# Eight column chunks by seven block products instead of five, each with its own operand distance, and accumulating DMAs for the low halves

## The chip, the core and the metric

The kernel runs on one core of a Trainium2 chip. The metric is the device time of one execution in microseconds (us), lower is better. A core has five engines with queues of their own: PE (TensorE, matrix products), DVE (VectorE), ACT (ScalarE), POOL (GpSimd) and SP (SyncE, which here issues DMAs). Each works through its queue in order; semaphores tie the queues together.

## The reference

One layer of a transformer block on 512 tokens of width 1024, in float32: two kinds of attention, an output projection, then a gated feed-forward part. The change concerns that last part alone:

```python
def conv_glu(x, w_up, conv_w, conv_b, w_down):      # x: 512 x 1024 (normalised)
    hid = x @ w_up                                   # 512 x 5632: 2816 gate, 2816 up columns
    hid = causal_depthwise_conv(hid, conv_w, width=3) + conv_b
    gate, up = hid[..., :2816], hid[..., 2816:]
    return (jax.nn.silu(gate) * up) @ w_down         # 2816 x 1024
```

## The kernel before

Float32 products are made of three matmuls each: both operands are split into a high part (`hi`, rounded to the fast fp32r type) and a low part (`lo`, the rest), and hi·hi, hi·lo and lo·hi are added up in PSUM.

**The up projection** runs in 22 chunks, `up0` to `up21`. A chunk holds 128 gate and 128 up columns; its weights are stationary, the transposed tokens (`hth`, `htl`) move. A chunk of the old form (`up_body`) takes 2 × 8 products of K = 128 with 512 moving columns, times three: 48 matmuls. A chunk named in `SEVEN` takes another way (`up_seven`): its weights and the tokens are seen as 2 × 2 blocks, and seven block products of 256 moving columns (4 × 3 matmuls each, 84 in all) stand for the eight, as in Strassen's scheme. The sums of token blocks (`ts`, four tiles) are made once; the sums of weight blocks are made for each such chunk by DVE in `block_sums` (tile `sx`) and split in `split_seven` into `wxh` and `wxl`. The products `p1`, `p5`, `p7`, `p6` leave by copies (`pc`, `hg`) and adds (`hu`, `hg`), which also set free the PSUM banks that the next chunk starts in.

The tiles of stationary weights (`whi`, `wlo`, `wxh`, `wxl`) are a little larger than needed, so that their used part can begin some elements behind the tile's start: 16 elements (64 bytes) for the sevens and for up0 and up1, 48 for some chunks of the attention, 0 for the rest. What is called the distance here is where the stationary operand starts minus where the moving one starts, modulo 256 bytes.

**The pairs.** The outputs of two chunks form a pair, 11 in all; a pair's blocks and their sums become the stationary operands of the down projection, `ax` (2048 wide: 1024 high, 1024 low) and `ay` (1536 wide: 768 and 768). `pair_sums(i)` makes four sums on DVE (into `st`, a tile with one buffer, and back into `ub`), then `halves` makes each high half by a copy on ACT (L908) and each low half by a subtraction on DVE (L909), in pieces of 768, 256, 256 and 512 columns. There is room for eight `ax`, but not for all `ay`: those of pairs 0 to 6 are stored to DRAM (`ayd`, L933, POOL's DMA queue) and fetched later by `fetch` (L953, also POOL). `ax8` lies in a `ts` buffer and `ay8` in the one of `wxh`, once the last seven is done.

**The down projection** takes 11 chunks `dn0_i` (which use `ax`) and then 11 `dn1_i` (which use `ay`); their weights are split in the same way, and their body runs `steps0` or `steps1` on the side: the sums of the last two pairs and fetches.

**What sets the order.** `run_chunk` interleaves a chunk's products with the split of the next chunk's weights (`split_gen`), piece by piece. The weights of the chunk after next are loaded (SP, 1 MB into one of two `raw` buffers) when a split ends; if the next chunk but one is a seven, its `block_sums` follow. A scheduler orders each engine's queue from the dependencies.

Of the kernel before, what the change touches and what calls it, by code (L numbers as in the profile page):

```python
# [8 lines left out]
F32 = mybir.dt.float32  # L9
F32R = mybir.dt.float32r  # L10
AF = mybir.ActivationFunctionType
ALU = mybir.AluOpType
# [3 lines left out]
P = 128  # L16
S = 512
# [42 lines left out]

CHUNKS = _chunks()

SEVEN = (5, 8, 11, 14, 17)


@with_exitstack
def block_kernel(ctx: ExitStack, tc: tile.TileContext, x, xt, params, g2, rbx, wts, wd0, wd1, out):
    nc = tc.nc
    V, A, G, PE, SP = nc.vector, nc.scalar, nc.gpsimd, nc.tensor, nc.sync
# [39 lines left out]
    raws, splits, late = {}, {}, {"halves": (), "casts": (), "products": ()}  # L109
    FIRST_DN = order.index("dn0_0")  # L110
    keep = {}
# [58 lines left out]
    def is_seven(i):  # L170
        return i < len(order) and order[i] in [f"up{j}" for j in SEVEN]

# [15 lines left out]
    def split_seven(i, raw, hi, lo):  # L188

        key = order[i]  # L190
        wh, wl = (late["pool"].tile([P, 1600], F32R, tag=tag, name=f"{tag}_{key}")[:, 16:1552]
                  for tag in ("wxh", "wxl"))
        splits[key] = tuple(t.rearrange("p (k c) -> p k c", c=P) for t in (hi, lo, wh, wl))
        sx = late["sx"]
        for j, (h, l, src) in enumerate(((hi[:, 0:1024], lo[:, 0:1024], raw[:, 0:1024]),
                                         (wh[:, 0:1024], wl[:, 0:1024], sx[:, 0:1024]),
                                         (hi[:, 1024:2048], lo[:, 1024:2048], raw[:, 1024:2048]),
                                         (wh[:, 1024:1536], wl[:, 1024:1536], sx[:, 1024:1536]))):
            A.copy(h, src)
            V.tensor_tensor(l, src, h.bitcast(F32), op=ALU.subtract)  # L200
            if j < 3:
                yield

    def split_gen(i, pieces):

        if i >= len(order):
            return
        key = order[i]
        kn = CHUNKS[i][1]
        raw = raws.pop(i)  # L210
        sh = 48 if key[:2] in ("qA", "kA", "vA", "vB") else 16 if key in ("up0", "up1") or is_seven(i) else 0
        n = 512 * kn if i >= FIRST_DN else 2048
        hi = wp.tile([P, 2112], F32R, tag="whi", name=f"whi_{key}")[:, sh:sh + n]
        lo = wp.tile([P, 2112], F32R, tag="wlo", name=f"wlo_{key}")[:, sh:sh + n]
        splits[key] = (hi.rearrange("p (k c) -> p k c", k=kn), lo.rearrange("p (k c) -> p k c", k=kn))
        if i >= FIRST_DN:
            yield from split_down(i - FIRST_DN, raw, hi, lo)
        elif is_seven(i):
            yield from split_seven(i, raw, hi, lo)
        n = 2048 // pieces  # L220
        for j in range(pieces if i < FIRST_DN and not is_seven(i) else 0):
            sl = slice(n * j, n * (j + 1))
            if i == 0 and j == 0:
                V.tensor_copy(hi[:, sl], raw[:, sl])
            else:
                A.copy(hi[:, sl], raw[:, sl])  # L226
            E = G if i == 2 else V
            E.tensor_tensor(lo[:, sl], raw[:, sl], hi[:, sl].bitcast(F32), op=ALU.subtract)  # L228
            if j < pieces - 1:
                yield  # L230


        nxt = {0: None, 1: i + 3, 2: None}.get(i - FIRST_DN, i + 2)
        if nxt is not None and nxt < len(order):
            next(load(nxt))
        yield
        if is_seven(i + 1):
            yield from block_sums(i + 1)
# [3 lines left out]
    def run_chunk(key, body, pieces=4):  # L242

        sp = split_gen(pos[key] + 1, pieces)
        for _ in body(*splits.pop(key)):
            next(sp, None)
            yield
        for _ in sp:
            pass
# [12 lines left out]
    pp = ctx.enter_context(tc.tile_pool(name="pp", bufs=1, space=PSUM))  # L262
    dram = ctx.enter_context(tc.tile_pool(name="dram", bufs=1, space=bass.MemoryType.DRAM))
    htd = dram.tile([NT, 2, P, S], F32, tag="htd", name="htd")
    ayd = dram.tile([7, P, 1536], F32, tag="ayd", name="ayd")


    reset = pool_c.tile([P, S], F32, tag="reset", name="reset")
# [560 lines left out]
    hi, lo = splits.pop("wo3")  # L829
# [8 lines left out]
    fp = late["pool"] = ctx.enter_context(tc.tile_pool(name="fp", bufs=1))  # L838
# [5 lines left out]
    pairs = {}  # L844
# [19 lines left out]
    def gate(j, pg):  # L864
        g = fp.tile([P, S], F32, tag="cg", name=f"cg{j}", bufs=1)
        conv(pg, j, g)
        A.activation(g, g, AF.Silu)
        return g

    def pair_sums(i):  # L870

        u0, u1 = ub[:, 2 * i % 4, :], ub[:, 2 * i % 4 + 1, :]
        u = ub[:, 2 * i % 4:2 * i % 4 + 2, :].rearrange("p a b -> p (a b)")
        lo_, hi_ = slice(0, 256), slice(256, 512)
        t = {}
        if i < 8:
            ax = fp.tile([P, 2048], F32R, tag="ax", name=f"ax{i}", bufs=8)
            ay = fp.tile([P, 1536], F32R, tag="ay", name=f"ay{i}")
        elif i == 8:

            ax = fp.tile([P, 2048], F32R, tag="ts", name=f"ax{i}", bufs=4)
            ay = fp.tile([P, 1600], F32R, tag="wxh", name=f"ay{i}")[:, 0:1536]
            keep[0] = fp.tile([P, S], F32, tag="hg", name="t2_0")
        else:

            ax = late["hp"].tile([P, 2048], F32R, tag=f"ax{i}", name=f"ax{i}")
            ay = late["hp"].tile([P, 1536], F32R, tag=f"ay{i}", name=f"ay{i}")
        pairs[i] = (ax, ay)

        def sums():  # L890
            t["st"] = st = fp.tile([P, 768], F32, tag="st", name=f"st{i}", bufs=1)
            s1, s42 = st[:, 0:256], st[:, 256:768]
            if i == 9:

                s42 = fp.tile([P, S], F32, tag="cg", name="s42_9", bufs=1)
            s4, s2 = s42[:, 0:256], s42[:, 256:512]
            t["s42"] = s42
            ins = [V.tensor_tensor(s1, u0[:, hi_], u1[:, hi_], op=ALU.add),
                   V.tensor_tensor(u0[:, hi_], u0[:, lo_], u0[:, hi_], op=ALU.subtract),
                   V.tensor_tensor(s2, s1, u0[:, lo_], op=ALU.subtract),  # L900
                   V.tensor_tensor(s4, u1[:, lo_], s2, op=ALU.subtract)]
            return ins

        def halves(a, parts):
            ins, n = [], a.shape[-1] // 2
            for o, src in parts:
                sl = slice(o, o + src.shape[-1])
                A.copy(a[:, sl], src)  # L908
                ins.append(V.tensor_tensor(a[:, n + o:n + sl.stop], src, a[:, sl].bitcast(F32), op=ALU.subtract))  # L909
            return ins  # L910
        return (sums, lambda: halves(ax, ((0, u[:, 0:768]), (768, t["st"][:, 0:256]))),
                lambda: halves(ay, ((0, u[:, 768:1024]), (256, t["s42"]))))

    def keep_place(i):
# [8 lines left out]
    def up_fin(j, pg, pu, g=None):  # L923
        if g is None:
            g = gate(j, pg)
        u = ub[:, j % 4, :]
        conv(pu, NF + j, u)
        late["fin"] = (V.tensor_tensor(u, g, u, op=ALU.mult),)
        if j % 2 == 1 and j // 2 < 9:
            for step in pair_sums(j // 2):  # L930
                step()
            if j // 2 < 7:
                G.dma_start(ayd[j // 2], pairs[j // 2][1].bitcast(F32))  # L933

    def up_body(j):
        def body(hi, lo):
# [10 lines left out]

    def fetch(i):

        tag = {0: "sx", 1: "wxl"}.get(i, "ts" if i < 5 else "ax")  # L950
        n, bufs = {"sx": (1536, 1), "wxl": (1600, 1), "ts": (2048, 4), "ax": (2048, 8)}[tag]
        ay = fp.tile([P, n], F32R, tag=tag, name=f"ay{i}", bufs=bufs)[:, 0:1536]
        G.dma_start(ay, ayd[i])  # L953
        pairs[i] = (pairs[i][0], ay)
# [3 lines left out]
    ts = {}  # L958
# [92 lines left out]
    for j in range(NF):  # L1051
        body = up_first(j) if j < 2 else up_seven(j) if j in SEVEN else up_body(j)
        for _ in run_chunk(f"up{j}", body, pieces=4 if j < 2 else 2):
            pass
        if j == 18:
            for i in range(5):
                fetch(i)


# [110 lines left out]
    def steps0():  # L1170
        yield
        for i in (9, 10):
            ss[i] = pair_sums(i)
            yield from late_pair(ss[i][:2])
            fetch(i - 4)

    def steps1():
        tmp["x"] = [fp.tile([P, 2, D], F32, tag="ax", name=f"x_{r}", bufs=8) for r in range(2)]
# [7 lines left out]
    for s in range(2):  # L1186
        steps = (steps0, steps1)[s]()
        for i in range(NP - 2 * s):
            for _ in run_chunk(f"dn{s}_{i}", down_body(s, i), pieces=2):
                pass  # L1190

    for _ in split_gen(pos[f"dn1_{NP - 1}"], 2):
        pass
# [13 lines left out]
def _layout(inputs):  # L1207
# [12 lines left out]
    for i, (key, kn, parts) in enumerate(CHUNKS[:-2 * NP]):  # L1220
        views = [f[name][0][r0:r0 + kn * P, c0:c0 + n] for name, r0, c0, n in parts]
        w = views[0] if len(views) == 1 else np.concatenate(views, axis=1)
        if key in [f"up{j}" for j in SEVEN]:

# [26 lines left out]
```

## Time and profile before

| | |
|---|---|
| median of 3 runs | 726.53 us (726.07 to 726.63) |
| the profiled execution | 726.66 us, its span 724.9 us |
| granted clock of TensorE | 1.000 |
| up2 to up21 | 402.8 to 615.6 us of the span |
| dn0_0 to the end | from 615.6 us |
| DMA in all | 100.9 MB, 139 GB/s over the span |

Busy times of an engine are sums of durations of its instructions. Since matmuls are pipelined, one lasts longer than the distance to the next one's start. A row of the page's groups gives line, engine, operation, output and inputs, shapes and count, then busy us and mean ns, then the idle time ahead and what ended it. A row of a timeline gives start, duration, engine and line. The chain that ended last tells which work the end of the span hung on.

### The profile page before, as it was taken

The page shows a single profiled execution, that of the slowest core. Times are in us where ns is not written, and L with a number is a line of the kernel's source. Part 1 is how long each engine was busy: PE and PEld are TensorE (multiplying, and loading weights), DVE is VectorE, ACT ScalarE, POOL GpSimd, SP SyncE. Part 2 cuts the span into 40 slices and gives each one's busy share as a digit, 9 for nine tenths or more (in the row PEclk, how much of TensorE's full clock was granted, in tenths as well). Part 3 has the DMA queues.
Part 4 walks back from the last instruction along what each step waited for, and adds up shares of the span by engine and source line. Part 5 has one row for each costly group of instructions (what it writes and reads, how often), then busy time and mean ns, then how long its engine had stood idle before and what let it go on. Part 6 is the DMA issues. An engine that isn't in the chain of part 4 may idle for free.

```text
span 724.9 us, 10589 instructions
## 1 busy us (share of the span) xinstructions
PE 718.6 (99%) x4019; PEld 627.5 (87%) x4019; DVE 565.4 (78%) x1030; ACT 401.5 (55%) x727; POOL 53.6 (7%) x95
## 2 busy tenths in 40 slices
PE   8999999999999999999999999999999999999997
PEld 8999998888988888888889889889898988888886
DVE  6678867775988888566275799998979985997686
ACT  6675656657767676442254556655545653543541
POOL 2701200000101011000012000000000100000000
PEclk9999999999999999999999999999999999999999
DMA  8632232211313111314536613544335553564563
GB/s 308 250 131 78 83 117 74 74 59 58 118 63 113 59 59 59 136 68 144 195 149 239 203 62 156 186 135 160 118 145 186 181 184 117 173 243 174 177 222 116
DMA packets 24786, 100.91 MB, mean 139 GB/s; under 512 B 2592, under 2 KB 7328, under 8 KB 17184
## 3 DMA queue, kind: packets, MB, share of 16 engines
q1 hardware_dynamic: 21792, 87.00, 33.8%
q0 software_dynamic: 2656, 13.11, 5.0%
q8 instruction: 31, 0.51, 0.3%
q14 instruction: 19, 0.16, 0.1%
q10 hardware_dynamic: 288, 0.14, 0.1%
HBM read 88.44 MB, written 11.80 MB: 138 GB/s over the span
## 4 chain that ended last, share of the span: by engine, by line
PE 98%; DMA 1%; SPq 0%; DVE 0%; ACT 0%; DVEq 0%; issue 0%
PE P L1087 14%; PE p L998 7%; PE pg L254 4%; PE pg L253 4%; PE pg L255 4%; PE pu L254 4%; PE pu L255 4%; PE pu L253 4%; PE qkB L255 2%; PE gB L255 2%; PE qkB L253 2%; PE gA L253 2%; PE gA L254 2%; PE gB L253 2%; PE gA L255 2%; PE qkB L254 2%
## 5 line engine op out<-in xcount | busy, mean ns | idle before, releaser
L253 PE MATMUL pg<-hth,whi_up 128*128 128x512 f32 (+1 forms) x152 | 55.7, 367 | 0.0
L255 PE MATMUL pg<-hth,wlo_up 128*128 128x512 f32 (+1 forms) x152 | 55.7, 366 | 0.0
L254 PE MATMUL pg<-htl,whi_up 128*128 128x512 f32 (+1 forms) x152 | 55.7, 366 | 0.0
L254 PE MATMUL pu<-htl,whi_up 128*128 128x512 f32 (+1 forms) x152 | 55.6, 366 | 0.0
L253 PE MATMUL pu<-hth,whi_up 128*128 128x512 f32 (+1 forms) x152 | 55.6, 366 | 0.0
L255 PE MATMUL pu<-hth,wlo_up 128*128 128x512 f32 (+1 forms) x152 | 55.6, 365 | 0.0
L1087 PE MATMUL P<-whi_dn,ax 128*128 128x512 f32 x176 | 54.4, 389 | 0.0
L149 ACT CAST whi_dn<-raw_dn 128x1024 fp32r<-128x1024 f32 x33 | 34.3, 1051 | 25.5 <-PE P L1087 15.2
L145 DVE TENSOR_TENSOR wlo_dn<-raw_dn,whi_dn 128x1024 fp32r<-128x1024 f32 x33 | 40.0, 1224 | 9.2 <-ACT whi_dn L149 9.1
L228 DVE TENSOR_TENSOR wlo_up<-raw_up,whi_up 128x1024 fp32r<-128x1024 f32 (+1 forms) x40 | 41.2, 1062 | 7.0 <-ACT whi_up L226 7.0
L226 ACT CAST whi_up<-raw_up 128x1024 fp32r<-128x1024 f32 (+1 forms) x40 | 34.5, 917 | 14.7 <-PE pu L254 7.9
L1087 PE MATMUL P<-whi_dn,ay 128*128 128x512 f32 x132 | 40.8, 389 | 0.0
L1087 PEld LDWEIGHTS P<-whi_dn,ax 128*128 128x128 f32 x176 | 33.0, 188 | 6.8
L1087 PE MATMUL P<-wlo_dn,ax 128*128 128x512 f32 x88 | 34.2, 389 | 0.0
L254 PEld LDWEIGHTS pu<-htl,whi_up 128*128 128x128 f32 x152 | 28.6, 188 | 4.7
L253 PEld LDWEIGHTS pu<-hth,whi_up 128*128 128x128 f32 x152 | 28.5, 188 | 4.7
L255 PEld LDWEIGHTS pg<-hth,wlo_up 128*128 128x128 f32 x152 | 28.6, 188 | 4.7
L255 PEld LDWEIGHTS pu<-hth,wlo_up 128*128 128x128 f32 x152 | 28.5, 188 | 4.6
L253 PEld LDWEIGHTS pg<-hth,whi_up 128*128 128x128 f32 x152 | 28.6, 188 | 4.6
L254 PEld LDWEIGHTS pg<-htl,whi_up 128*128 128x128 f32 x152 | 28.6, 188 | 4.5
L633 DVE TENSOR_TENSOR_SCAN aB<-aB,reset 128x127 f32<-128x127 f32 (+3 forms) x32 | 26.0, 817 | 6.7 <-ACT aB L628 6.7
L1087 PEld LDWEIGHTS P<-whi_dn,ay 128*128 128x128 f32 x132 | 24.8, 188 | 5.1
(303 smaller groups left out, 2240.3 us busy)
## 6 DMA issues: line engine op xcount, KB each, us to landing
raw_up<-in_wts SPq DMA_DIRECT2D x22, 1024.0 KB, 4.8
raw_dn<-in_wd SPq DMA_DIRECT2D x11, 1024.0 KB, 4.8
raw_dn<-in_wd SPq DMA_DIRECT2D x11, 512.0 KB, 3.4
ayd<-ay POOLq DMA_DIRECT2D x7, 768.0 KB, 5.2
ay<-ayd POOLq DMA_DIRECT2D x7, 768.0 KB, 6.5
raw_gA<-in_wts SPq DMA_DIRECT2D x4, 1024.0 KB, 4.7
raw_qkB<-in_wts SPq DMA_DIRECT2D x4, 1024.0 KB, 4.8
raw_gB<-in_wts SPq DMA_DIRECT2D x4, 1024.0 KB, 4.7
```

Source lines behind the costliest of these rows:

```text
L145: chain("halves", V.tensor_tensor(o, x, y, op=op))
L149: chain("casts", A.copy(hi[:, sl], src))
L226: A.copy(hi[:, sl], raw[:, sl])
L228: E.tensor_tensor(lo[:, sl], raw[:, sl], hi[:, sl].bitcast(F32), op=ALU.subtract)
L253: PE.matmul(ps, sh, mh, start=first, stop=False)
L254: PE.matmul(ps, sh, ml, start=False, stop=False)
L255: PE.matmul(ps, sl, mh, start=False, stop=last)
L633: V.tensor_tensor_scan(ar, ar, reset[:, S - n:S - 1][:, ::-1], 1.0, op0=ALU.mult, op1=ALU.max)
L998: PE.matmul(ps, st, mv[:, k, :], start=first and k == 0 and n == 0, stop=last and k == 3 and n == 2, skip_group_check=True)
L1087: chain("products", PE.matmul(dst, st, mv, start=first and n == 0, stop=last and n == 2, skip_group_check=True))
```

## The change

`SEVEN` goes from five chunks to eight, every second one from up8 on. Each has its own shift of the stationary operand in its tile, from 4 to 56 elements (`BEHIND`, 16 to 224 bytes); chunks that aren't sevens keep theirs. In the built program all moving operands of these products start at one place modulo 256 bytes, and so do the tiles of the stationary ones, so that the shift is the distance.

The low halves of pairs 0 to 8 are no longer subtracted by DVE: ACT writes −src, rounded to fp32r, into the low half's place (that is minus the high half), and a DMA on POOL's queue with `accum_op=add` adds src to it. That makes four such DMAs per pair, 36 in all, of 128, 128, 256 and 384 KB.

With more sevens the `ts`, `wxh` and `sx` tiles are in use until up20, so that buffers move: pair 8 gets an `ax` and an `ay` buffer like the others; for that `ax0` is stored to DRAM (`axd`, 1 MB) and reloaded into a `ts` buffer after up20, and `ay7` is stored too. The fetches come after up20 (0 and 1), after the down chunks 1, 3, 5, 7, 9 (2, 6, 7, 3, 4) and after dn1_0 (5). In code:

```diff
-SEVEN = (5, 8, 11, 14, 17)
+SEVEN = (5, 8, 10, 12, 14, 16, 18, 20)
+BEHIND = dict(zip(SEVEN, (4, 8, 12, 20, 24, 28, 40, 56)))
 def split_seven(i, raw, hi, lo):
-    wh, wl = (late["pool"].tile([P, 1600], F32R, tag=tag, name=f"{tag}_{key}")[:, 16:1552]
+    sh = BEHIND[int(key[2:])]
+    wh, wl = (late["pool"].tile([P, 1600], F32R, tag=tag, name=f"{tag}_{key}")[:, sh:sh + 1536]
...
-    sh = 48 if key[:2] in ("qA", "kA", "vA", "vB") else 16 if key in ("up0", "up1") or is_seven(i) else 0
+    sh = 48 if key[:2] in ("qA", "kA", "vA", "vB") else 16 if key in ("up0", "up1") else BEHIND[int(key[2:])] if is_seven(i) else 0
...
-    ayd = dram.tile([7, P, 1536], F32, tag="ayd", name="ayd")
+    ayd = dram.tile([8, P, 1536], F32, tag="ayd", name="ayd")
+    axd = dram.tile([P, 2048], F32, tag="axd", name="axd")
...
 def pair_sums(i):
-        if i < 8:
+        if i < 9:
             ax = fp.tile([P, 2048], F32R, tag="ax", name=f"ax{i}", bufs=8)
             ay = fp.tile([P, 1536], F32R, tag="ay", name=f"ay{i}")
-        elif i == 8:
-            ax = fp.tile([P, 2048], F32R, tag="ts", name=f"ax{i}", bufs=4)
-            ay = fp.tile([P, 1600], F32R, tag="wxh", name=f"ay{i}")[:, 0:1536]
-            keep[0] = fp.tile([P, S], F32, tag="hg", name="t2_0")
...
+                lo = a[:, n + o:n + sl.stop]
                 A.copy(a[:, sl], src)
-                ins.append(V.tensor_tensor(a[:, n + o:n + sl.stop], src, a[:, sl].bitcast(F32), op=ALU.subtract))
+                if i < 9:
+                    A.activation(lo, src, AF.Copy, scale=-1.0)
+                    G.dma_start(lo, src, accum_op=ALU.add)
+                else:
+                    ins.append(V.tensor_tensor(lo, src, a[:, sl].bitcast(F32), op=ALU.subtract))
...
-            if j // 2 < 7:
+            if j // 2 < 8:
                 G.dma_start(ayd[j // 2], pairs[j // 2][1].bitcast(F32))
+            if j // 2 == 6:
+                G.dma_start(axd, pairs[0][0].bitcast(F32))
...
     def fetch(i):
-        tag = {0: "sx", 1: "wxl"}.get(i, "ts" if i < 5 else "ax")
+        tag = {0: "sx", 1: "wxl", 2: "wxh"}.get(i, "ts" if i < 6 else "ax")
...
-        if j == 18:
-            for i in range(5):
+        if j == SEVEN[-1]:
+            keep[0] = fp.tile([P, S], F32, tag="hg", name="t2_0")
+            ax0 = fp.tile([P, 2048], F32R, tag="ts", name="ax0_", bufs=4)
+            G.dma_start(ax0, axd)
+            pairs[0] = (ax0, None)
+            for i in range(2):
                 fetch(i)
...
-            fetch(i - 4)                      # in steps0
...
+            n = ({1: 2, 3: 6, 5: 7, 7: 3, 9: 4}, {0: 5})[s].get(i)
+            if n is not None:                 # behind each chunk of the down projection
+                fetch(n)
```

Three places show what this makes of the queues. First POOL's queue at pair 0, as it stands now; `ay0<-ub`, `ax0<-st0` and the like are accumulations into the low half, `axd` and `ayd` the places in DRAM:

```order
L912 DMA ay0_4439<-ub_4185 128x256
L912 DMA ax0_4438<-st0_4440 128x256
L912 DMA ax0_4438<-ub_4185 128x768
L941 DMA axd_109<-ax0_4438 128x2048
L912 DMA ay0_4439<-st0_4440 128x512
L938 DMA ayd_108<-ay0_4439 128x1536
L912 DMA ax1_4604<-st1_4606 128x256
```

Before, only the store `ayd<-ay0` stood there, with that of pair 1 right behind it. The store of ax0, written for pair 6 in the code, now stands ahead of pair 0's last accumulation, the one that reads `st0`.

Second DVE's queue in up5, before; `st1` is the tile of pair 1's sums, `p6_5` the bank of up5's product p6:

```order
L1010 TENSOR_TENSOR pc5_4697<-pc5_4697 128x256
L854 SCALAR_TENSOR_TENSOR ub_4184<-pu4_4621,par_88,ub_4184 128x510
L1013 TENSOR_TENSOR hu5_4699<-p6_5_4696,pc5_4697 128x256
L898 TENSOR_TENSOR st1_4601<-ub_4184 128x256
L909 TENSOR_TENSOR ay1_4600<-ub_4184,ay1_4600 128x256
L853 SCALAR_TENSOR_TENSOR cg4_4654<-pg4_4620,par_88,cg4_4654 128x511
L899 TENSOR_TENSOR ub_4184<-ub_4184 128x256
```

And the same place of the changed kernel:

```order
L858 SCALAR_TENSOR_TENSOR ub_4185<-pu4_4630,par_88,ub_4185 128x510
L1018 TENSOR_TENSOR pc5_4706<-pc5_4706 128x256
L897 TENSOR_TENSOR st1_4606<-ub_4185 128x256
L1021 TENSOR_TENSOR hu5_4708<-p6_5_4705,pc5_4706 128x256
L857 SCALAR_TENSOR_TENSOR cg4_4663<-pg4_4629,par_88,cg4_4663 128x511
L898 TENSOR_TENSOR ub_4185<-ub_4185 128x256
```

The subtractions into `ay1` are gone from the queue, and the first sum of pair 1, which writes `st1` into the one buffer that `st0` had, stands ahead of the add that reads `p6_5`; it stood behind it.

Third POOL's queue from pair 8 on, now; `ax0_` is the reloaded tile:

```order
L912 DMA ay8_6061<-ub_4185 128x256
L961 DMA ay0_6394<-ayd_108 128x1536
L912 DMA ax8_6060<-st8_6062 128x256
L912 DMA ax8_6060<-ub_4185 128x768
L912 DMA ay8_6061<-st8_6062 128x512
L1066 DMA ax0__6392<-axd_109 128x2048
L961 DMA ay3_6793<-ayd_108 128x1536
L961 DMA ay4_6865<-ayd_108 128x1536
L961 DMA ay2_6560<-ayd_108 128x1536
L961 DMA ay1_6396<-ayd_108 128x1536
```

Behind these stand the fetches of ay5, ay6 and ay7. Before, no accumulations and no reload stood here: the fetches ran from ay0 to ay6 in order, with the store of ay6 behind the fetch of ay0. Now the fetch of ay0, which waits for the `sx` buffer, stands among pair 8's accumulations.

More of the change, by code (lines that the diff above doesn't have):

```diff
@@ L948, in fetch @@
     def fetch(i):
-        tag = {0: "sx", 1: "wxl"}.get(i, "ts" if i < 5 else "ax")
-        n, bufs = {"sx": (1536, 1), "wxl": (1600, 1), "ts": (2048, 4), "ax": (2048, 8)}[tag]
+        tag = {0: "sx", 1: "wxl", 2: "wxh"}.get(i, "ts" if i < 6 else "ax")
+        n, bufs = {"sx": (1536, 1), "wxl": (1600, 1), "wxh": (1600, 1), "ts": (2048, 4), "ax": (2048, 8)}[tag]
         ay = fp.tile([P, n], F32R, tag=tag, name=f"ay{i}", bufs=bufs)[:, 0:1536]
```

## The prediction

> **What bounds the kernel now.** I read the page first: the busy times of the engines and the chain that ended last.
>
> ```profile
> span 724.9 us, 10589 instructions
> PE 718.6 (99%) x4019; PEld 627.5 (87%) x4019; DVE 565.4 (78%) x1030; ACT 401.5 (55%) x727; POOL 53.6 (7%) x95
> PE 98%; DMA 1%; SPq 0%; DVE 0%; ACT 0%; DVEq 0%; issue 0%
> ```
>
> TensorE (PE) is busy for 99% of the span and is 98% of the chain. So the time changes by what PE's own stream gets shorter, plus every hole that opens in it. Next I read the up projection alone, from the start of up2 to the start of the down projection, as the sums of one window.
>
> ```profile
> core 0: us, PE busy (x) PEld busy (x) DVE busy (x) ACT busy (x) POOL busy (x), PEclk, DMA share, GB/s
> 402.80:615.60 212.80, 212.80 (x1142) 184.65 (x1141) 188.08 (x283) 117.18 (x172) 6.45 (x12) 1.00 0.43 151
> ```
>
> Here PE has no hole at the window's resolution, at a granted clock of 1.00. VectorE (DVE) is busy 188.08 of 212.80 us, 88%; ScalarE (ACT) 55%. DVE is the engine that could become late.
>
> **The term that shortens PE.** The durations of matmuls are pipelined, so I take distances between starts, from PE's timeline: start, duration, line. The rows are the first of up5 (a seven), the first of up6 and the first of up7 (both of the old form), and the first of up8.
>
> ```profile
> 435.44 0.28 PE L998 MATMUL p<-hth,whi_up 128*128 128x256 f32 x1
> ...
> 445.33 0.40 PE L253 MATMUL pg<-hth,whi_up 128*128 128x512 f32 x1
> ...
> 456.24 0.39 PE L253 MATMUL pg<-hth,whi_up 128*128 128x512 f32 x1
> ...
> 467.12 0.28 PE L998 MATMUL p<-hth,whi_up 128*128 128x256 f32 x1
> ```
>
> A seven takes 445.33 − 435.44 = 9.89 us for 84 matmuls, 117.7 ns each. The 48 matmuls of 512 columns take 467.12 − 456.24 = 10.88 us (226.7 ns each), and 10.91 right behind a seven, so each return costs 0.03. A chunk that becomes a seven saves 10.88 − 9.89 − 0.03 = 0.96 us. Five become eight: **−2.88 us**.
>
> **The distances.** All five sevens of before have one distance, 64 bytes (16 elements); the change gives 16, 32, 48, 80, 96, 112, 160 and 224. The trace shows no run of matmuls at any of these. What it shows is that the rate at 64 bytes itself isn't one number. In the last part of up1, the same distance, 256 columns:
>
> ```profile
> 395.74 0.28 PE L255 MATMUL pu<-hth,wlo_up 128*128 128x256 f32 x1
> 395.86 0.28 PE L253 MATMUL pu<-hth,whi_up 128*128 128x256 f32 x1
> ...
> 396.76 0.28 PE L255 MATMUL pu<-hth,wlo_up 128*128 128x256 f32 x1
> ```
>
> Nine steps in 1.02 us are 113.3 ns each, against 117.7 in the sevens. So something of 4.4 ns per matmul lies between equal distances. If every new distance ran at 113.3, the eight sevens would win 8 × 84 × 4.4 ns = 3.0 us more. As the other end I take the same step upward, 122.1 ns: 3.0 us lost. The value I take is **0**: each of the five sevens, at different places and with different neighbours, ran at 117.7, and these are the nearest rows. Both ends stay in the range.
>
> **DVE and ACT.** For pairs 0 to 8 the subtraction that makes the low half goes from DVE to an ACT activation and an accumulating DMA from POOL. The groups of the stretch 435 to 615 us, forms apart (count, busy, mean ns of one):
>
> ```profile
> L909 DVE TENSOR_TENSOR ax<-ub,ax 128x768 fp32r<-128x768 f32 x9 | 8.6, 955 | 0.0
> L909 DVE TENSOR_TENSOR ay<-st,ay 128x512 fp32r<-128x512 f32 x9 | 6.2, 689 | 0.0
> L909 DVE TENSOR_TENSOR ay<-ub,ay 128x256 fp32r<-128x256 f32 x8 | 3.4, 424 | 0.0
> L909 DVE TENSOR_TENSOR ax<-st,ax 128x256 fp32r<-128x256 f32 x8 | 3.4, 420 | 0.0
> L908 ACT CAST ax<-ub 128x768 fp32r<-128x768 f32 x8 | 6.7, 834 | 2.7 <-DVE ub L899 2.7
> L908 ACT CAST ay<-st 128x512 fp32r<-128x512 f32 x9 | 5.6, 620 | 5.7 <-DVE st L901 5.7
> L908 ACT CAST ay<-ub 128x256 fp32r<-128x256 f32 x8 | 3.2, 406 | 6.8 <-DVE ub L928 6.8
> L908 ACT CAST ax<-st 128x256 fp32r<-128x256 f32 x8 | 3.2, 401 | 3.8 <-DVE st L898 3.8
> ```
>
> DVE loses 955 + 689 + 424 + 420 = 2.49 us per pair, 22.4 over nine. ACT gains a second pass of the same forms, 834 + 620 + 406 + 401 = 2.26, 20.3 over nine. Three more sevens add work to both: on DVE four block sums, two low halves of the sums and five short adds each, on ACT two casts and four short copies.
>
> ```profile
> L179 DVE TENSOR_TENSOR sx_up<-raw_up 128x512 f32<-128x512 f32 x4 | 2.8, 688 | 2.9 <-DMA raw_up<-in_wts 2.9
> L200 DVE TENSOR_TENSOR wxl_up<-sx_up,wxh_up 128x1024 fp32r<-128x1024 f32 x4 | 4.9, 1225 | 0.0
> L200 DVE TENSOR_TENSOR wxl_up<-sx_up,wxh_up 128x512 fp32r<-128x512 f32 x4 | 2.8, 690 | 0.0
> L1019 DVE TENSOR_TENSOR hg<-p,hu 128x256 f32<-128x256 f32 x5 | 2.1, 423 | 1.1 <-PE p L998 1.1
> L199 ACT CAST wxh_up<-sx_up 128x1024 fp32r<-128x1024 f32 x4 | 4.2, 1040 | 1.8 <-DVE sx_up L181 1.8
> ```
>
> Per seven DVE gets 4 × 0.69 + 1.225 + 0.69 + 5 × 0.42 = 6.8 us, 20.3 for three: 188.1 − 22.4 + 20.3 = 186.0 of about 210, 89%. ACT gets 1.04 + 0.62 + 4 × 0.40 (casts of 512 and 256 columns, as in the rows before) = 3.3 per seven, so 117.2 + 20.3 + 9.8 = 147, 70%. Both are hidden behind PE: **0** on the sum. Without the move DVE would need 208 of 210 us, and that cover would be gone.
>
> **The accumulating DMAs.** 36 of them come in, four per pair, with 128 KB to 384 KB each; the trace of before has none. The plain transfers:
>
> ```profile
> raw_up<-in_wts SPq DMA_DIRECT2D x22, 1024.0 KB, 4.8
> raw_dn<-in_wd SPq DMA_DIRECT2D x11, 512.0 KB, 3.4
> ayd<-ay POOLq DMA_DIRECT2D x7, 768.0 KB, 5.2
> L933 POOL DMA_DIRECT2D ayd<-ay x7 | 3.7, 535 | 134.0 <-DVE ay L909 73.9 <-DVE cg L853 45.9 <-DVE pc L1010 14.2
> ```
>
> 512 KB more cost 1.4 us, so about 2.0 us are fixed. At the price of a copy, the accumulations last 2.35, 2.35, 2.7 and 3.05 us (an estimate from these rows); that is the lower end. As the upper end I take twice the moving part and the same start, 2.7, 2.7, 3.4 and 4.1, and for a queue that serves them badly, more. POOL itself spends 0.54 us on an issue: 5 per pair are 2.7 us in two chunks, no bound.
>
> What an accumulation can hold up is the one `st` buffer. The next pair's first sum on DVE must not write it before the last accumulation of this pair has read it. Behind that sum on DVE stands, in up5, the add `hu5<-p6_5` that frees the bank for the first product of up6. DVE's timeline in up5 today:
>
> ```profile
> 435.23 0.96 DVE L909 TENSOR_TENSOR ax<-ub,ax 128x768 fp32r<-128x768 f32 x1
> ...
> 443.80 0.43 DVE L1013 TENSOR_TENSOR hu<-p,pc 128x256 f32<-128x256 f32 x1
> 444.13 0.43 DVE L898 TENSOR_TENSOR st<-ub 128x256 f32<-128x256 f32 x1
> ```
>
> In the built program the two have changed places: `st` first, `hu` behind. For pair 0 POOL holds: the accumulation of 768 columns, the 1 MB store of ax0 (which waits for it), then the accumulation `ay<-st`. If the 768 columns start where their subtraction ended, 436.2, they land at 439.2; the store is issued at 439.7, `ay<-st` at 440.3. It lands at 443.0 if the store doesn't hold it, and at 440.3 + 2.7 + 2.8 = 445.8 if the store's moving part goes first. PE wants up6's bank at 445.33, about 0.8 us after the sum may begin: a hole of 0 to 1.3 us. With twice the moving part, both accumulations add 1.05 + 0.7: up to 3.0. I take **+1.0** here, near the end with the store ahead.
>
> **Loads of the next weights.** A seven's block sums wait for its raw weights, whose load is issued only when an older chunk is split; sevens in every second chunk leave less room. A load beside several POOL transfers was late: the load rows of two windows with such transfers (552.8 to 560.5, and 572.5 to 588.5), and the longest wait for a load, from DVE's timeline:
>
> ```profile
> raw_up<-in_wts SPq DMA_DIRECT2D x1, 1024.0 KB, 7.0
> raw_up<-in_wts SPq DMA_DIRECT2D x1, 1024.0 KB, 8.8
> 541.20 0.69 DVE L179 TENSOR_TENSOR sx_up<-raw_up 128x512 f32<-128x512 f32 x1 [2.90 <-DMA raw_up<-in_wts]
> ```
>
> DVE stood still for 2.90 us there, and PE had no hole. That cover is about 3 us; I take **0** for the loads, and up to 2 us at each of about three places (up16, up20, the first down chunks) if accumulations fill the queues. The fetches that move from the end of up18 to between the down chunks land long before their use: 0; the reload of ax0 (1 MB, 4.8 us by the load's row) stands beside them.
>
> **The sum.** The profiled execution took 726.66 us (its span and 1.8 us around it), 0.13 over the median of 726.53. 726.66 − 2.88 + 0 + 0 + 1.0 + 0 = 724.78; less 0.13 is **724.7 us**.
>
> **Rivals.**
> (a) *All of it covered, or the distances help*: no hole at up6 gives 723.7; with 113.3 ns everywhere 720.7. For it: equal distances show both rates. Against: every seven so far ran at the slower one.
> (b) *The distances cost*: some make two operands collide. At 122.1 ns for all, 724.7 + 3.0 = 727.7; at half of it 726.2. That the change does nothing (gain eaten) lies here. For it: a rate does vary by 4 ns. Against: nothing in the trace ties it to a distance.
> (c) *Slower: accumulations at twice a copy's moving part or worse*, at the `st` buffer and in the queues that the weight loads share. Up to 3.0 us at up6, and at three later places 1.5 to 2 each: 726.53 − 2.88 + 3.0 + 4.5 = 731.2. It decides from about 2.9 us of holes in all, and holes begin when `ay<-st` lands after 444.5 or a load takes over about 7.3. For it: a pair's accumulations move 896 KB, which beside a 768 KB store and two loads is 3.6 MB in 20.8 us, 175 GB/s on average, and bursts like those that made loads take 7.0 and 8.8; at double, 4.5 MB. Against: before's 151 GB/s left PE whole.
> The Trainium skill, "Collectives: The Full Stack", section "The bandwidth ceiling: the fold count and why AG ≠ RS ≠ AR", says that an add in the DMA path needs two source reads and so ran at about half the rate of a copy. No run here shows it yet; by it (c) would be the case, 731 instead of 724.7.
>
> **Chances.** Forecast (723.6 to 725.0) 0.36; (a) 0.10; (b), 725.1 to 728.0, 0.20; (c) 0.34. A measurement of this kernel tells about 0.2% (1.45 us) from no change, so faster is below 725.08: 0.46; same 0.20; slower 0.34. The range from 720.7 (all distances fast) to 731.5 (just over (c)'s price) leaves out about 0.17, mostly above. Signs are mixed: the forecast's own range is 723.6 to 725.0.
>
> **What would show it.** Distances: starts within each of the eight sevens, 9.89 us each if I am right; a seven of 9.5 or 10.2 shows a distance that counts. The hole: PE's start of up6 against the last matmul of up5, and whether DVE's wait is for a POOL transfer of `st`. Accumulations: issue to landing by size, 2.4 to 3.1 if like a copy. Loads: raw_up's median and its longest against 4.8 and 8.8. DVE busy near 186 us in the stage and ACT near 147. I am wrong if the eight sevens differ from 9.89 by over 0.1 on average, if holes in the stage exceed 2 us, or if PE waits in the down projection.

## The result and the profile after

The changed kernel takes 764.72 us (median of 4 runs, 761.04 to 766.66), the kernel before 726.30 us beside it (4 runs, 725.87 to 726.63). The ratio is 1.0523, 95% interval 1.048 to 1.0567: 38 us slower, where 724.7 was forecast. One execution of run f4 below, the profiled one, took 1464.18 us against 726.41 to 729.17 in its other ten; f4's figures leave it out. The page of the changed kernel, the lines that answer to those of before:

```profile
span 764.2 us, 10995 instructions
PE 729.6 (95%) x4127; PEld 639.0 (84%) x4127; DVE 565.5 (74%) x1027; ACT 424.2 (56%) x781; POOL 87.0 (11%) x135
PE 15%; DMA 4%; ACT 3%; DVE 3%; issue 2%; DVEq 0%; ACTq 0%; POOLq 0%; SPq 0%
```

PE is no longer what the end hangs on all the way: the chain that could be followed runs through DMAs, ACT and DVE too. PE is idle for 764.2 − 729.6 = 34.6 us where it was 6.3 before, and its busy time is 11.0 us longer, though its stream should take 2.9 us less. So 28.3 us are holes, and 13.9 us are matmuls that took longer. The windows show where both lie (time; busy us of PE, PEld, DVE, ACT, POOL; granted clock; DMA share; GB/s):

```profile
402.80:650.20 247.40, 223.55 (x1261) 197.89 (x1261) 188.19 (x281) 139.58 (x225) 39.67 (x52) 0.95 0.60 170
500.00:550.00 50.00, 46.01 (x272) 41.88 (x273) 41.35 (x64) 31.29 (x53) 8.26 (x11) 0.90 0.55 153
550.00:600.00 50.00, 42.88 (x251) 38.68 (x250) 39.20 (x62) 29.85 (x51) 7.73 (x10) 0.93 0.57 160
```

In the up projection, now until 650.2, PE idles for 23.9 us and the granted clock is 0.95; no engine is near its limit (DVE 188 of 247 us). Four of the longest waits of the same stretch say who waits for whom (us in total, times, longest):

```profile
ACT ay L908 <- DMA ayd<-ay: 39.9, 6, 11.9
DVE st L897 <- DMA ay<-st: 21.3, 5, 5.1
POOL ayd L938 <- DMA ay<-st: 18.2, 4, 6.3
PE p L1006 <- ACT pc L1011: 13.0, 5, 3.6
```

The first row is new: before, ACT had no wait for a store. ACT stands still for 39.9 us because the high half of the next pair's `ay` may be written only when the store of this pair's `ay` has landed: `ay` has one buffer. POOL's timeline of one pair shows why the store is late (start, duration, idle time ahead), and the DMA view of the stretch 497 to 514 us gives the landings:

```profile
497.65 0.85 POOL L912 DMA_DIRECT2D ay<-ub  x1 [4.21 <-ACT ay L911]
500.65 0.84 POOL L912 DMA_DIRECT2D ax<-st  x1 [2.15 <-DVE hu L1031]
503.67 0.86 POOL L912 DMA_DIRECT2D ax<-ub  x1 [2.17 <-ACT whi_up L202]
508.76 0.85 POOL L912 DMA_DIRECT2D ay<-st  x1 [4.23 <-issue]
514.11 0.57 POOL L938 DMA_DIRECT2D ayd<-ay  x1 [4.50 <-DMA ay<-st]
521.77 0.84 POOL L912 DMA_DIRECT2D ay<-ub  x1 [7.09 <-ACT ay L911]
```

```profile
ax<-ub POOLq DMA_DIRECT2D x1, 384.0 KB, 4.8
ay<-st POOLq DMA_DIRECT2D x1, 256.0 KB, 4.7
ay<-ub POOLq DMA_DIRECT2D x1, 128.0 KB, 2.7
ax<-st POOLq DMA_DIRECT2D x1, 128.0 KB, 2.7
```

497.65 + 2.7 is 500.35, and the next accumulation is issued at 500.65; 500.65 + 2.7 = 503.35, the next at 503.67; 503.67 + 4.8 = 508.5, the next at 508.76. **Each accumulation is issued 0.3 us after the one before has landed.** Over the whole trace this holds for 22 of the 35 steps from one accumulation to the next (0.31 to 0.35 us); in the other 13 it was later, in none earlier. The engines named in brackets are not what the last three waited for: ACT's passes into their low halves had ended at 497.85, 500.27 and 502.53, 2.8 to 6.2 us before the issues. Nor does the program hold them back: in the trace none of the 35 issues waits for the semaphore by which the accumulation before signals its landing. So a pair needs four accumulations, one store and the next pair's passes on ACT, all in series, 24.1 us from 497.65 to 521.77, where PE needs 20.8 us for its two chunks. The four landings are 14.9 us of it, the store 6.4. From 426.43 to 621.53, over eight pairs, a turn took 24.4 us on average. The loop sets the pace.

How it reaches PE: ACT works in order, so what is queued behind the waiting cast comes late. The next pair, in ACT's timeline (three rows) and in PE's (four):

```profile
545.36 0.41 ACT L908 CAST ay<-ub 128x256 fp32r<-128x256 f32 x1 [5.96 <-DMA ayd<-ay]
...
557.04 0.78 ACT L855 ACTIVATE ub<-pu,par 128x512 f32<-128x512 f32 x1
557.71 0.37 ACT L1011 COPY pc<-p 128x256 f32<-128x256 f32 x1
```

```profile
554.67 0.28 PE L1006 MATMUL p<-ts,wxl_up 128*128 128x256 f32 x1
558.13 0.58 PE L1006 MATMUL p<-hth,whi_up 128*128 128x256 f32 x1 [3.18 <-ACT pc L1011]
...
561.29 0.41 PE L1006 MATMUL p<-hth,wxl_up 128*128 128x256 f32 x1
561.50 0.32 PE L1006 MATMUL p<-hth,wxh_up 128*128 128x256 f32 x1
```

ACT loses 5.96 us, then works through its backlog until the copy that frees a bank of PE, and PE waits 3.18 us. And PE comes back at half speed: from 558.13 to 561.50 a matmul of 256 columns lasts 0.41 us instead of 0.28. The granted clock was 0.50 there (the third figure from the row's end):

```profile
558.15:561.57 3.42, 3.42 (x16) 3.42 (x17) 3.42 (x5) 1.44 (x4) 0.86 (x1) 0.50 0.41 74
```

That is the second price of a hole. The Trainium skill, "TensorE: Matmul & The Clock Gate", section "What's actually happening", says that the array's clock is halved after an idle window of about 3.4 us and given back after about as long a busy one; the 3.4 us at half speed here agree. The hole ahead of them, 3.18 us, is a little shorter than such a window; a hole of 2.81 us brought 3.4 us at 0.50 in the profiled execution of e1 and none in that of e4.

### The profile page after: what moved, and what is told of

Read it like the earlier page. It is cut to its first block, busy times and chain, and to the rows that moved or that the text cites. A ratio compares the mean times of both kernels' runs of the same rounds, so it can differ in the third digit from the quotient of the medians.

```text
span 764.2 us, 10995 instructions
## 1 busy us (share of the span) xinstructions
PE 729.6 (95%) x4127; PEld 639.0 (84%) x4127; DVE 565.5 (74%) x1027; ACT 424.2 (56%) x781; POOL 87.0 (11%) x135
## 5 line engine op out<-in xcount | busy, mean ns | idle before, releaser
L256 PE MATMUL pg<-hth,whi_up 128*128 128x512 f32 (+1 forms) x128 | 47.2, 369 | 2.9 <-DVE hu L1021 2.9
L258 PE MATMUL pg<-hth,wlo_up 128*128 128x512 f32 (+1 forms) x128 | 47.1, 368 | 0.0
L257 PE MATMUL pg<-htl,whi_up 128*128 128x512 f32 (+1 forms) x128 | 46.9, 366 | 0.0
L257 PE MATMUL pu<-htl,whi_up 128*128 128x512 f32 (+1 forms) x128 | 46.3, 362 | 0.0
L256 PE MATMUL pu<-hth,whi_up 128*128 128x512 f32 (+1 forms) x128 | 46.3, 362 | 0.0
L258 PE MATMUL pu<-hth,wlo_up 128*128 128x512 f32 (+1 forms) x128 | 46.3, 361 | 0.0
L1006 PE MATMUL p<-hth,whi_up 128*128 128x256 f32 x64 | 20.9, 327 | 18.6 <-ACT pc L1011 13.0
L231 DVE TENSOR_TENSOR wlo_up<-raw_up,whi_up 128x1024 fp32r<-128x1024 f32 (+1 forms) x34 | 34.0, 1028 | 3.0 <-ACT whi_up L229 3.0
L908 ACT CAST ay<-ub 128x256 fp32r<-128x256 f32 x11 | 4.5, 406 | 48.6 <-DMA ayd<-ay 39.9
L1006 PEld LDWEIGHTS p<-hth,whi_up 128*128 128x128 f32 x64 | 14.0, 219 | 20.6 <-ACT pc L1011 14.0
L639 POOL TENSOR_SCALAR_AFFINE_SELECT bB<-bB 128x128 f32<-128x128 f32 x32 | 13.6, 428 | 149.1 <-DVE bB L638 134.4
L256 PEld LDWEIGHTS pg<-hth,whi_up 128*128 128x128 f32 x128 | 24.4, 191 | 6.7 <-DVE hu L1021 3.1
L258 PEld LDWEIGHTS pg<-hth,wlo_up 128*128 128x128 f32 x128 | 24.4, 190 | 4.0
```

The lines of the kernel that those rows point to most:

```text
L256: PE.matmul(ps, sh, mh, start=first, stop=False)
L257: PE.matmul(ps, sh, ml, start=False, stop=False)
L258: PE.matmul(ps, sl, mh, start=False, stop=last)
L639: G.affine_select(b[:, n - P:n], b[:, n - P:n], pattern=[[-1, P]], compare_op=ALU.is_gt, fill=0.0, base=0, channel_multiplier=1)
L1006: PE.matmul(ps, st, mv[:, k, :], start=first and k == 0 and n == 0, stop=last and k == 3 and n == 2, skip_group_check=True)
```

## The experiments

Four theories were tried. **A**: accumulations run one after another and close the loop described above. **B**: the new distances slow the matmuls. **C**: sevens in every second chunk leave loads and block sums too little room. **D**: it is the bytes on POOL's queue or the one `ay` buffer, whatever the kind of DMA.

**e1_dve_halves**: the changed kernel without accumulations.

```diff
-                if i < 9:
+                if False:
                     A.activation(lo, src, AF.Copy, scale=-1.0)
                     G.dma_start(lo, src, accum_op=ALU.add)
                 else:
                     ins.append(V.tensor_tensor(lo, src, a[:, sl].bitcast(F32), op=ALU.subtract))
```

> The changed kernel, but the low halves of pairs 0 to 8 made by DVE's subtraction again: no accumulating DMA is left; eight sevens, the eight distances and the moved fetches stay. Theory A (the accumulations run one after another on POOL's queue and, with the one ay buffer, form a loop of about 24.4 us per pair where PE needs 20.8): the holes in PE and the lowered clock go, DVE stands near its limit (208 of 210 us in the stage), 723 to 729 us. Theory B (the new distances slow the matmuls): still above 755. Theory C (sevens in every second chunk leave the weight loads and block sums too little room, whoever makes the halves): holes stay ahead of the sevens, 735 to 755.

Measured: 730.08 us (729.0 to 731.73), ratio 1.005 (1.0033 to 1.0067). 34.6 of the 38 us are gone with the accumulations, B falls, and C keeps at most the rest. It is still above A's range: one hole of 2.8 us is left, in the down projection (below, e4).

**e2_all_64**: the changed kernel with one distance.

```diff
-BEHIND = dict(zip(SEVEN, (4, 8, 12, 20, 24, 28, 40, 56)))
+BEHIND = dict(zip(SEVEN, (16,) * 8))
```

> The changed kernel with one distance of 64 bytes for all eight sevens instead of eight different ones, all else kept. Theory A: no change that counts, 760 to 768. Theory B: the sevens go back to 9.89 us each and the time to 723 to 730. Theory C: as A, 760 to 768.

Measured: 764.55 us (764.37 and 764.72), as the changed kernel. The distances are not the cause.

**e3_before_acc**: the kernel before, with accumulations.

```diff
                 A.copy(a[:, sl], src)
-                ins.append(V.tensor_tensor(a[:, n + o:n + sl.stop], src, a[:, sl].bitcast(F32), op=ALU.subtract))
+                if i < 9:
+                    A.activation(a[:, n + o:n + sl.stop], src, AF.Copy, scale=-1.0)
+                    G.dma_start(a[:, n + o:n + sl.stop], src, accum_op=ALU.add)
+                else:
+                    ins.append(V.tensor_tensor(a[:, n + o:n + sl.stop], src, a[:, sl].bitcast(F32), op=ALU.subtract))
```

> The kernel before (five sevens, 64 bytes, fetches where they were), with one edit: the low halves of pairs 0 to 8 by an ACT pass and an accumulating DMA. Theory A: two chunks take PE 21.1 us on average here, the loop still about 24, so holes of 2 to 4 us per pair and a lowered clock: 745 to 765. Theories B and C: nothing they speak of is in it, 726 to 730.

Measured: 757.76 us, ratio 1.0436 (1.0388 to 1.0484). This edit alone, with five sevens and the old distances, costs 32 us. Its longest wait in the up projection is the same one:

```profile
ACT ay L908 <- DMA ayd<-ay: 41.0, 5, 10.7
```

**e4_dve_64**: e1 with 64 bytes everywhere.

> As e1_dve_halves, and all eight distances 64 bytes. Theory A with distances that don't matter: within 1 us of e1_dve_halves. If the distances matter by what the medians of the changed kernel's trace say (117 to 122 ns, 130 at 48 bytes), e4 is 1 to 2 us faster than e1. Theory C: like e1, 735 to 755.

Measured: 729.75 us (728.31 to 731.65), 0.33 from e1, within their spread. The sevens' gain went in the only wait that PE has from 402 us on, for DVE's last convolution of up21, whose bank the down projection takes over:

```profile
PE P L1099 <- DVE cg L858: 2.8, 1, 2.8
```

That DVE is late there because the subtractions came back to it while three more sevens load it is what f2 below supports. So of C about 3 us are left, through DVE, not 38. The profiled execution was also late before this stage: its up5 began at 437.42 us against 435.44 before (last section).

**e5_plain_copies**: the changed kernel with plain copies, which leave the addition out.

```diff
-                    G.dma_start(lo, src, accum_op=ALU.add)
+                    G.dma_start(lo, src.bitcast(F32R))
```

> The changed kernel with each of the 36 accumulating DMAs replaced by a plain copy of the same bytes between the same tiles; it leaves the addition out, so the low halves hold the whole number. Theory A (an accumulating DMA holds back the next one until it has landed): plain copies are issued one behind the other, 0.55 us apart where nothing else is waited for, and the time falls to 723 to 730 us. Theory D (the bytes that POOL's queue moves, or the one ay buffer alone, make the loop too long, whatever the kind of DMA): still above 745.

Measured: 729.92 us (728.91 and 730.92). The same number of DMAs, the same bytes, tiles, queue and `ay` buffer, and 35 us are gone: D falls. The copies also read their source as fp32r, where the accumulations read float32 into fp32r; that this change of type alone holds nothing back is seen in the changed kernel's fetches, plain DMAs from float32 into fp32r tiles: one was issued at 638.44 and landed at 646.23, the next was issued at 638.98. POOL's timeline at one place, and the DMA view of 478 to 482 us:

```profile
478.75 0.54 POOL L912 DMA_DIRECT2D ay<-ub  x1 [5.57 <-DVE ub L898]
479.36 0.53 POOL L912 DMA_DIRECT2D ax<-st  x1
```

```profile
ax<-ub POOLq DMA_DIRECT2D x1, 384.0 KB, 2.6
ay<-ub POOLq DMA_DIRECT2D x1, 128.0 KB, 2.0
ax<-st POOLq DMA_DIRECT2D x1, 128.0 KB, 2.0
```

A copy is issued 0.61 us behind another one that takes 2.0 us to land. Of the 35 steps 18 came before the landing of the one before, against none of 35 with accumulations. Single transfers hardly lasted less: a pair's four landings and its store add up to 21.5 us on average here, to 21.9 in the changed kernel, but here they overlap. Alone on the queue a copy is shorter (2.0, 2.0, 2.3 and 2.6 us against 2.7, 2.7, 3.3 and 3.9), so copies one after another might take 24.1 − 3.7 = 20.4 us a pair, an estimate from these rows and just under PE's 20.8. That series of copies was not run, so how the 35 us divide between the order and the longer transfers stays open. ACT's wait for the store of `ay` is down to 3.2 us:

```profile
ACT ay L908 <- DMA ayd<-ay: 3.2, 2, 1.9
```

**e6_ax_acc_64**: e2 with accumulations for `ax` alone.

```diff
-                if i < 9:
+                if i < 9 and n == 1024:
```

> The changed kernel at 64 bytes, with only the low halves of ax (pieces of 768 and 256 columns) by accumulating DMAs; those of ay by DVE. Theory A: two accumulations of some 2.7 to 6 us per pair no longer close the loop through the ay buffer within 20.8 us; no holes in the up projection, and DVE is relieved of 1.4 us per pair: 724 to 728. Theory D or a price that goes with the count of accumulations: half of the 38 us lost, about 745.

Measured: 730.05 us (729.54 to 731.97). Half of the accumulations cost not half of the 38 us but at most a few (e4, with none, took 729.75), so the price does not go with their count. It is above A's range: PE waited 2.4 us once for a convolution on DVE near 495 us, with 3.4 us at a granted clock of 0.50 behind it. What made DVE late there was not tried.

**e7_ay_acc_64**: e2 with accumulations for `ay` alone.

```diff
-                if i < 9:
+                if i < 9 and n == 768:
```

> The changed kernel at 64 bytes, with only the low halves of ay (pieces of 256 and 512 columns) by accumulating DMAs; those of ax by DVE. Here the two accumulations and the store stay in the loop that frees the one ay buffer. Theory A: 2.7 to 5.6, 0.3, 3.3 to 7, then 3.6 to 6 for the store come to 10 to 19 us, under the 20.8 that PE gives a pair, so no lasting loss: 726 to 732. A price that goes with the count of accumulations in that loop, below its period too: 740 or more.

Measured: 725.32 us (10 runs, 724.86 to 726.84), before 725.95 beside it, ratio 0.9995 (0.9986 to 1.0004). The loop through `ay` is here, but with two accumulations it is shorter than the period. POOL's timeline of one pair:

```profile
502.02 0.87 POOL L912 DMA_DIRECT2D ay<-ub  x1 [9.04 <-ACT ay L911]
508.98 0.85 POOL L912 DMA_DIRECT2D ay<-st  x1 [6.09 <-DVE ub L858]
512.85 0.56 POOL L938 DMA_DIRECT2D ayd<-ay  x1 [3.02 <-DMA ay<-st]
522.82 0.84 POOL L912 DMA_DIRECT2D ay<-ub  x1 [9.41 <-ACT ay L911]
```

The next pair starts after 20.80 us, the period of PE, and POOL waits for data instead of the others for POOL. In the up projection nothing is lost, and DVE is relieved of 1.1 us per pair. PE's starts of up5 and of the down projection are now 177.28 us apart:

```profile
435.97 0.28 PE L1006 MATMUL p<-hth,whi_up 128*128 128x256 f32 x1
...
613.25 0.39 PE L1099 MATMUL P<-whi_dn,ax__6374 128*128 128x512 f32 x1
```

Before, it was 615.62 − 435.44 = 180.18 us (the down projection's first row is here):

```profile
615.62 0.39 PE L1087 MATMUL P<-whi_dn,ax 128*128 128x512 f32 x1
```

So three more sevens do save 2.90 us when nothing is late. Of these, 1.6 us arrive at the end of the profiled execution (span 723.3 us against 724.9): up5 began 0.5 us later than before, and the down projection took 0.8 us more, for reasons that stay open. By the interval above, e7 cannot be told from the kernel before.

**e8_ay_acc_224**: e7 with another distance.

```diff
-BEHIND = dict(zip(SEVEN, (16,) * 8))
+BEHIND = dict(zip(SEVEN, (56,) * 8))
```

> As e7_ay_acc_64, with 224 bytes for all eight sevens instead of 64. In e1_dve_halves and e5_plain_copies the one seven at 224 bytes (up20) ran at 116.7 ns per matmul, against 117.8 at 64 bytes. If that is the distance: all eight sevens take 9.80 us instead of 9.89 and the time falls by 0.7 us to 724.6. If it was the place of up20: 9.89 in the others, and 725.3.

Measured: 724.99 us (11 runs, 724.19 to 726.96), before 726.12, ratio 0.9987 (0.9978 to 0.9996): the one version of those tried that is faster than the kernel before, by 0.13%, with the interval's end just under 1. The rate of the sevens is set by the distance, not by the place of the chunk. The first matmul of up10 and the first behind it, in e8 and then in e4 at 64 bytes:

```profile
489.50 0.28 PE L1006 MATMUL p<-hth,whi_up 128*128 128x256 f32 x1
...
499.30 0.40 PE L256 MATMUL pg<-hth,whi_up 128*128 128x512 f32 x1
```

```profile
489.91 0.28 PE L1006 MATMUL p<-hth,whi_up 128*128 128x256 f32 x1
...
499.80 0.40 PE L256 MATMUL pg<-hth,whi_up 128*128 128x512 f32 x1
```

9.80 us against 9.89, that is 116.65 and 117.8 ns per matmul. Seven of e8's eight sevens take 9.80 in the profiled execution; up8 has a hole of 1.6 us in it, and the medians of e7 and e8 are 0.3 apart, not 0.7.

**f1 to f4** looked for a version that beats both without accumulations. f1, the kernel before with two sevens more:

```diff
-SEVEN = (5, 8, 11, 14, 17)
+SEVEN = (5, 7, 9, 11, 13, 15, 17)
```

> The kernel before with one line changed: SEVEN = (5, 7, 9, 11, 13, 15, 17), seven chunks instead of five, 64 bytes, subtractions on DVE, no spill of ax0. Each added seven saves 0.96 us if DVE keeps up, as the up projection of e4_dve_64 did: 726.07 - 1.92 = 724.2, and up18 to up21 give DVE time to catch up before the down projection's first banks are needed. If DVE falls behind for good: 726 to 729.

Measured: 727.60 us, ratio 1.0024 (1.0015 to 1.0034). PE waits 0.55 us for DVE's add `hu` at up6, and 1.26 us near 551 us for a cast of the block sums on ACT: together 1.8 of the 1.92 us that two sevens should save. Why it is 1.6 us slower than the kernel before on top of that is open.

f2, e4 with the 768-column subtraction of pairs 0 to 8 on POOL:

```diff
-                    ins.append(V.tensor_tensor(lo, src, a[:, sl].bitcast(F32), op=ALU.subtract))
+                    ins.append((G if i < 9 and src.shape[-1] == 768 else V).tensor_tensor(lo, src, a[:, sl].bitcast(F32), op=ALU.subtract))
```

> As e4_dve_64, but the largest low half of each pair (768 columns) is subtracted by POOL itself instead of DVE. DVE is relieved of 0.96 us per pair, so the hole of 3.0 us at the start of the down projection, where DVE's last convolution was late, should go: 725 to 727. If POOL and DVE hold each other up: 729 to 733.

Measured: 727.34 us, ratio 1.0018 (1.0009 to 1.0027). The hole at the start of the down projection is gone, which supports that DVE's lateness made it; three of 0.4 to 0.6 us stand at other places.

f3: f1 with the same subtraction on POOL.

> As f1_seven_to_17, and the 768-column low half of pairs 0 to 8 subtracted by POOL. DVE is relieved of 0.96 us per pair. If the two holes of f1 came from a late DVE: they go, 724 to 725. If they came from a late weight load: 726 to 728.

Measured: 727.72 us, ratio 1.0022 (1.0013 to 1.0031): f1's hole near 551 us is gone, the wait for `hu` at up6 is 1.2 us instead of 0.55, and this execution began late (last section).

f4: the kernel before with `SEVEN = (5, 8, 11, 13, 15, 17)` and the subtraction on POOL.

> The kernel before with six sevens (5, 8, 11, 13, 15, 17) and the 768-column low half of pairs 0 to 8 subtracted by POOL. One seven more saves 0.96 us: 725.1 if nothing is late.

Measured: 726.94 us, ratio 1.0019 (1.001 to 1.0028), not the 725.1 expected; where the gain went is open.

## Why the prediction was wrong

**The step that failed** is the one on accumulating DMAs. It priced a single accumulation, and it took POOL's part as "0.54 us on an issue: 5 per pair are 2.7 us in two chunks, no bound". That holds for copies (e5). An accumulation is issued only when the one before has landed, so POOL's part of a pair is the sum of four landings and the store, not the sum of five issues. Nothing in the trace of before could show it, since it has no accumulation. But the bounds were too narrow: "at twice the moving part" was made the upper end, and a queue that works off its transfers one by one was not among the cases, though the sum for it could be made from the rows at hand: 2.35 + 2.35 + 3.05 + 2.7 and 5.2 for the store are 15.7 us at a copy's price, and 7 or 8.8 us for a transfer beside others was a row. 15.7 us are still under PE's 20.8, so by these rows the order alone would not yet make a loss; measured, the four landings came to 14.9 us instead of 10.5 and the store to 6.4, and with the steps between them the turn to 24.1.

**The second miss** belongs to it: the text said "What an accumulation can hold up is the one `st` buffer". The one `ay` buffer is held longer, since the store waits for the accumulations, and ACT for the store. That wait alone is 39.9 us after, 3.2 us with plain copies.

**The `st` hole at up6** was right in mechanism, and mis-sized: +1.0 was taken, up to 3.0 for the dear case. It measured 2.88 us of wait on the `hu` add, DVE having stood 5.11 us for `ay<-st`, which landed at 450.80 where 443.0 to 445.8 was forecast; PE itself was 1.3 us late from the start and had waited 1.67 us at 442.6, or the hole would be larger:

```profile
450.92 0.42 DVE L897 TENSOR_TENSOR st<-ub 128x256 f32<-128x256 f32 x1 [5.11 <-DMA ay<-st]
...
451.73 0.50 PE L256 MATMUL pg<-hth,whi_up 128*128 128x512 f32 x1 [2.88 <-DVE hu L1021]
```

**The price of one accumulation** fits the upper bound. One of each size after the change that had the queue to itself:

```profile
ax<-st POOLq DMA_DIRECT2D x1, 128.0 KB, 2.7
ay<-st POOLq DMA_DIRECT2D x1, 256.0 KB, 3.3
ax<-ub POOLq DMA_DIRECT2D x1, 384.0 KB, 3.9
```

0.6 us per 128 KB, against (2.6 − 2.0) / 2 = 0.3 for e5's copies: the moving part is doubled. The rule that the Trainium skill, "Collectives: The Full Stack", section "The bandwidth ceiling: the fold count and why AG ≠ RS ≠ AR", states for an add between cores, two source reads and about half a copy's rate, agrees with these rows. Rival (c) had this price and the right sign, and 731.2 us; it lacked the series and the half clock.

**The sevens**: −2.88 was right, −2.90 in e7. **The distances**: 0 was taken, with 3.0 either way. In e1 and e5, without many holes, the eight ran at 118.3, 118.3, 118.3, 118.6, 117.4, 119.9, 119.9 and 116.7 ns (16 to 224 bytes in order; mean distance of a seven's starts), 118.4 on average against 117.8: +0.4 us in all. The bounds were too wide, the value right. **DVE and ACT**: 186 and 147 us were forecast for the stage; 188 and 140 were measured. But DVE at 95% (e4: 200 of 210 us) was not free of cost: 2.8 us at its end.

**The holes' second price** was not in the sum. Five stretches of the stage (from 452.34, 500.13, 558.15, 585.46 and 633.25 us), 23.9 us together, ran at a granted clock of 0.50, and PE was busy for 19.6 us of them; at a clock of 1.00 that work might have taken half. So about 10 of the 13.9 us by which the matmuls took longer are the clock's, an estimate from these numbers. The distances are 0.4, the rest is open.

## What to carry to other kernels

Before DMAs of a new kind take work off a busy engine, ask not only how long one lasts but whether the next may start before it has landed; if not, add up all that a buffer waits for, and compare it with the period of the loop. Below the period the chain costs nothing (e7), above it each turn costs the difference (24.4 − 20.8 = 3.6 us here), and on PE the half clock comes on top. An engine's busy time (POOL 11%) says nothing about such a chain.

## What the runs showed that was not expected

Accumulating DMAs are issued one at a time: 0.31 us or more after the landing of the one before, in all 35 steps of the changed kernel; also in e2 and e3 (35 each), e6, e7 and e8 (17 each). In the changed kernel no semaphore of the program makes them wait; whether the queue, the descriptors or something else does was not tried. A fetch and the reload of ax0 were issued 0.55 us behind an accumulation, so a plain DMA is not held in the same way.

The distance between the operands modulo 256 bytes moves the rate of matmuls of 256 columns a little: 116.65 ns at 224 bytes in seven sevens of e8, 117.8 at 64 bytes, about 119.9 at 112 and at 160. At 64 bytes all eight chunks ran alike (e7), at 224 seven of eight were measured (e8); each of the other distances was seen in one chunk alone. The second rate that the prediction saw at 64 bytes, 113.3 ns, came back in e6 behind a hole (474 to 477 us, in a chunk that had run at 117.8 ahead of it), so something besides the distance moves the rate too. Why is open.

The first products of the whole kernel started up to 3 us apart in profiled executions whose orders there are the same: the 101st matmul of PE at 17.15 us before, 16.78 in e3, 18.48 after the change, 19.59 in e4 and 19.97 in f3, where PE waited 2.3 us for the first weights' cast. This adds 1.3 us to the profile after, and blurs what one profiled execution can tell; what decides it was not tried.
